# A decoder layer on one core: gates and rotary key as high and low columns of one weight unit, constant rows by SyncE, half of the rope tables in the second block

## The chip, the core and the metric

The kernel runs on one core of a Trainium2 chip. The core has a matrix engine (TensorE, PE in the rows, with its weight loads PEld), a vector engine (VectorE, DVE), an activation engine (ScalarE, ACT), a general engine (GpSimd, POOL) and SyncE (SP), which here only issues DMAs. Each engine works off its own instructions in order. The metric is the device time of one execution in microseconds (us): the median of three runs of the kernel before is 2408.57 us (2407.36 to 2414.97).

## The reference, cut to what matters

One layer on 2048 tokens of width 1024, all in float32. Only the token mixer's first part is touched by the change:

```
a    = rmsnorm(x, g)
proj = a @ w_in          # columns: qk 512, v 512, o 512, gates 8, c_q 256, c_kv 128, k_r 32
gates = proj[gates] + b_gates                     # input and forget gates of 4 mLSTM heads
h_ml  = mlstm(silu(conv(qk)), v, gates) ...       # recurrent over chunks
k_rope = rope(k_r, cos, sin)                      # one rotary key, shared by 8 heads
q, k  = [nope | rope] per head from c_q, c_kv     # then causal attention, 8 heads
out   = x + norm(mix @ w_out) ...  then the MLP
```

rope(x1, x2) is (x1 cos - x2 sin, x1 sin + x2 cos) on the two 16-wide halves of the 32 values.

## The kernel before, in words

**Float32 in three products.** TensorE multiplies in the type fp32r. A float32 factor is split into a high part (its value rounded to fp32r, by an ACT copy) and a low part (what is left, by a subtraction). A product of two such factors is three matmuls into one PSUM bank: high by high, high by low, low by high (`mm3`, lines 252 to 255, which is why nearly all matmuls have the lines L253, L254, L255).

**The projection** runs in four blocks of 512 tokens. A block goes through units of 128 columns of w_in: 13 to 15 are the latents, 0 is a mixed unit, 1 to 4 the conv inputs, 5 to 8 the values, 9 to 12 the output gates, 16 to 18 the second projections of the latents (k, v, q and rotary q). Unit 0 holds 8 gate columns, 56 zero columns, 32 columns of the rotary key, and the same 32 with their halves exchanged. Eight steps k of mm3 (24 matmuls) fill its PSUM bank; `stabiliser` (line 960 on) takes it out as the tile G (128 x 512), transposes the 8 gate rows with four small matmuls (`gp`, L976) and starts the mLSTM's gate arithmetic. `rotate` (lines 921 to 959) multiplies the rotary key rows with the rope tables: a load of the table tile tg, three DVE operations (POOL in block 0), an ACT rounding, one more subtraction, two stores to krd in DRAM.

**Weights.** In block 0 a unit's raw columns are loaded (tile wr), split into wh and wl, and wl is stored to DRAM (wparts). In later blocks most units load wr and wl, and only wh is computed again, by ACT (`wload`).

**Rope tables** are computed on DVE and ACT in two halves (`rope_tables`, L1361 to L1392): half 0 serves blocks 0 and 2, half 1 blocks 1 and 3. `RB`, `RK` name the operation after which a half's positions are loaded; before, both start behind the last x tile of block 0.

**Towards attention.** The last block's four mLSTM chunks (num, hn, ht) run while the first attention work starts: score maxima m of head 0 need the tiles QK (row parts loaded from DRAM: qkd, qrd, krd), then the scores S with one more row, number 96, that is constant (one for K, zero for the low parts). These rows are loaded by DMAs that POOL issues (L1496, L1498) from the input `edge`, once for each of two QK tiles. POOL also fills the ones column of V (L1487, L1492) and a 65-column matrix onecol (L1493, L1494), and computes the pow of the mLSTM's norm (sm, L1289), the weighted q (qs, L1235) and some low parts of the probabilities (pl, L1668).

**Order.** A planner (`Plan.run`) simulates all operations with estimated costs, keys and buffer rings, and emits them in its order; on PE, ACT, DVE and POOL that order is pinned. On SP it is the order of issue. So an edit of one operation's cost or place moves many rows near it.

Of the kernel before, what the change touches and what calls it, by code (L numbers as in the profile page):

```python
# [54 lines left out]
OB = 1  # L55
QLO = 0
# [35 lines left out]
RB = (0, 0)  # L92
RK = (7, 7)
# [151 lines left out]
def trunk(ctx: ExitStack, tc: tile.TileContext, x, xT, pos, wu, wout, wup, wdn, cols, rows, consts, edge, out, dbg=None):  # L245
# [39 lines left out]
    identr = top.tile([P, P], F32R, tag="identr", name="identr")  # L285

# [4 lines left out]
    qrd = dram.tile([2, P, 2, SEQ], F32, tag="qrd", name="qrd")  # L291
    krd = dram.tile([32, 2, SEQ], F32, tag="krd", name="krd")
# [24 lines left out]
    for name, bufs in (  # L317
        ("awr", WR), ("wh", 5), ("wl", 5), ("mma", 1), ("mmb", 1), ("pst", 1), ("chh", 1), ("sg", SG), ("cbc", 1), ("G", GB_), ("raw", 2), ("cy", 2), ("cth", 2),
        ("rsbc", 2), ("tg", 1), ("R", 1), ("aS", 2), ("E", 2), ("iwbc", 1), ("qs", 1), ("num", 1), ("kv", 1), ("kw", 1), ("hn", HN),
        *((f"x{x}{k}", 2 if k < XDB else 1) for k in range(KD) for x in "hl"),  # L320
    ):
        pl.ring(name, bufs)
# [23 lines left out]
    mrow = b1.tile([1, 20], F32, tag="mrow", name="mrow")  # L346
    cst8 = [b1.tile([P, 129], F32, tag=f"C{p}", name=f"C{p}") for p in range(2)]
# [39 lines left out]
    o_rest = pl.op("SP", 1000, load_rest, [o_fill], key=kA(0, 16), kb=70)  # L387

    def fills2():
        for p in range(2):  # L390
            pool.memset(cst8[p], 0.0)
        pool.memset(vext[:, :, :, 128:129], 1.0)

# [3 lines left out]
    o_fill2 = pl.op("Pool", 900, fills2, key=kA(0, -40))  # L397
    pl.op("Activation", 600, masks, [o_rest], key=kA(1, 0))
# [46 lines left out]
    def wload(b, u):  # L445
# [10 lines left out]
        def place_l():  # L456
            t["l"] = wp.tile([P, 1024], F32R, tag="wl", name=f"wl{b}_{u}", bufs=5)
# [14 lines left out]
        o_turn[:] = [gl]  # L472
# [4 lines left out]

    def wsplit(b, u):
        if b > STB[u]:
# [16 lines left out]
        def lo(s):  # L496
            if s.start == 0:
                t["l"] = wp.tile([P, 1024], F32R, tag="wl", name=f"wl{b}_{u}", bufs=5)
# [38 lines left out]
    def unit(b, u):  # L537
# [5 lines left out]
        def mm(k):  # L543
            if k == 0:
                t["p"] = psm.tile([P, TB], F32, tag=t["at"], name=f"mm{b}_{u}")
            s = slice(k * P, (k + 1) * P)
            mm3(t["p"], w["h"][:, s], w["l"][:, s], *tiles[b, k], k == 0, k == KD - 1)

        last = None
        for k in range(KD):  # L550
            last = pl.op(
                "PE", PIN, lambda k=k: mm(k), [w["op"][k], *o_x[b, k]] + ([last] if k else behind), kA(b, TIME[b][u] + (FILL if k and fill else 0.0)),
# [371 lines left out]
    def rotate(b, t, G):  # L924
# [4 lines left out]
        def load():  # L929
            t["tgr"] = e2.tile([P, TB], F32R, tag="cth", name=f"tg{b}")  # L930
            t["tg"] = f32(t["tgr"])
            dma(t["tg"][64:128], trigd[:, b * TB : (b + 1) * TB])
# [18 lines left out]
        g = pl.op("SP", 500, load, [o_rope[b % 2], G], key, take=("cth",), kb=128)  # L951
        o = pl.op(*cost, d1, [g, G], key)
# [9 lines left out]
    def stabiliser(b):  # L962
# [10 lines left out]
        def gates():  # L973
            t["p"] = pst.tile([P, 512], F32, tag="tr", name=f"gp{b}")
            for c in range(4):
                pe.transpose(t["p"][:, c * 8 : c * 8 + 8], t["G"][0:8, c * P : (c + 1) * P], ident[0:8, 0:8])  # L976
# [104 lines left out]
        h = pl.op("PE", 330, gates, [G, o_cst], key, take=("pst",), free=[("G", G)])  # L1081
# [352 lines left out]
    a2 = av = ar2 = pq = pS = po = onecol = maskneg = None  # L1434
# [25 lines left out]
    def switch3():  # L1460

        nonlocal av, ar2, pS, po, onecol
# [8 lines left out]
        onecol = av.tile([P, P], F32R, tag="onecol", name="onecol")[:, 0:65]  # L1471
# [16 lines left out]
    for s in (0, "v", 1):  # L1488

        def fill(s=s):  # L1490
            if s == "v":
                pool.memset(f32(V[1][:, :, :, 128:129]), 1.0)  # L1492
                pool.memset(f32(onecol[:, 0:64]), 0.0)  # L1493
                pool.memset(f32(onecol[:, 64:65]), 1.0)  # L1494
            else:
                pool.dma_start(Kh[s][96:97, :], edge[0:1])  # L1496
                for z in (Kl, Ql):
                    pool.dma_start(z[s][96:97, :], edge[1:2])  # L1498

        o_const[s] = pl.op("Pool" if s == "v" else "SP", 490 if s == "v" else 1500, fill, [o_s3 if s else o_s1], key=EKEY - 30 if s == 0 else -50, kb=0 if s == "v" else 24)  # L1500
# [1186 lines left out]
def prepare(inputs):  # L2687
# [8 lines left out]
    z = np.zeros((DM, 56), np.float32)  # L2696
    misc = np.concatenate([w[:, 1536:1544], z, kr, kr[:, 16:], kr[:, :16]], axis=1)
# [68 lines left out]
```

## Time and profile before

| | us |
|---|---|
| median of 3 runs | 2408.57 (2407.36 to 2414.97) |
| the profiled execution's own time | 2408.7 |
| its span, first to last instruction | 2406.9 |
| PE busy in the span | 2360.4 (98%) |
| DVE, ACT, POOL busy | 1732.2, 1361.8, 815.3 |
| mean granted TensorE clock | 0.995 of full speed |
| mean DMA rate | 187 GB/s |

The projection takes about the first 480 us of the span, the change over to attention the next 60, attention, output projection and MLP the rest. A matmul's row gives the time from its start to a modelled end; matmuls overlap, so the distance from one start to the next is shorter than the duration in the row. A row of a timeline has the start, the duration (with "x8" that of eight merged instructions), engine, line, operation, output and inputs, and in brackets the idle time of the engine before it and what ended that. A row of the windows view has a stretch, its length, each engine's busy time in it, the granted clock, the DMA share and GB/s.

### The profile page before, as it was taken

The page shows a single profiled execution, that of the slowest core. Times are in us where ns is not written, and L with a number is a line of the kernel's source. Part 1 is how long each engine was busy: PE and PEld are TensorE (multiplying, and loading weights), DVE is VectorE, ACT ScalarE, POOL GpSimd, SP SyncE. Part 2 cuts the span into 40 slices and gives each one's busy share as a digit, 9 for nine tenths or more (in the row PEclk, how much of TensorE's full clock was granted, in tenths as well). Part 3 has the DMA queues.
Part 4 walks back from the last instruction along what each step waited for, and adds up shares of the span by engine and source line. Part 5 has one row for each costly group of instructions (what it writes and reads, how often), then busy time and mean ns, then how long its engine had stood idle before and what let it go on. Part 6 is the DMA issues. An engine that isn't in the chain of part 4 may idle for free. (4 is left out here: it accounts for less than half of the span.)

```text
span 2406.9 us, 34273 instructions
## 1 busy us (share of the span) xinstructions
PE 2360.4 (98%) x11141; PEld 1904.2 (79%) x11141; DVE 1732.2 (72%) x3105; ACT 1361.8 (57%) x2644; POOL 815.3 (34%) x698
## 2 busy tenths in 40 slices
PE   9999999989999999999999999999999999999997
PEld 7777878767777777788788888888888888888885
DVE  6867665658888888647767677766675677776777
ACT  5646454437778877444666556655564344433454
POOL 2725242538788888422000000000000223222346
PEclk9999999999999999999999999999999999999998
DMA  8697979886222321567777797665674445445358
GB/s 288 217 336 248 351 249 335 267 197 152 54 56 54 81 57 32 160 225 249 243 214 221 226 310 221 203 171 167 191 218 139 147 135 181 124 149 164 127 140 164
DMA packets 341308, 449.22 MB, mean 187 GB/s; under 512 B 34908, under 2 KB 227432, under 8 KB 341128
## 3 DMA queue, kind: packets, MB, share of 16 engines
q1 hardware_dynamic: 337192, 440.16, 58.7%
q0 software_dynamic: 3936, 6.87, 2.0%
q8 instruction: 88, 1.44, 0.3%
q14 instruction: 92, 0.75, 0.1%
HBM read 295.97 MB, written 153.05 MB: 187 GB/s over the span
## 5 line engine op out<-in xcount | busy, mean ns | idle before, releaser
L2575 POOL TENSOR_TENSOR y<-vd_0X,y 128x512 f32<-128x512 f32 x7 | 10.6, 1519 | 726.5 <-ACT vd_0X L2572 726.5
L1660 ACT ACTIVATE ph<-S 128x512 fp32r<-128x512 f32 (+1 forms) x320 | 170.3, 532 | 86.7 <-PE S L255 49.9
L1695 POOL TENSOR_TENSOR t<-t,ph 128x512 f32<-128x512 f32 (+1 forms) x192 | 212.9, 1109 | 17.3 <-ACT ph L1660 6.8
L2487 ACT CAST hh<-hr 128x512 fp32r<-128x512 f32 (+1 forms) x208 | 116.2, 567 | 157.0 <-PE d_5X L2538 15.4
L1668 DVE TENSOR_TENSOR pl<-S,ph 128x512 fp32r<-128x512 f32 (+3 forms) x271 | 156.4, 589 | 31.8 <-ACT S L1664 28.9
L253 PE MATMUL mm<-xh,wh 128*128 128x512 f32 x384 | 156.5, 408 | 4.2 <-DVE gate L1185 2.2
L2492 DVE TENSOR_TENSOR hl<-hr,hh 128x512 fp32r<-128x512 f32 (+1 forms) x208 | 133.0, 646 | 30.0 <-ACT hh L2487 23.5
L1601 DVE TENSOR_REDUCE mp<-m 128x1 f32<-128x512 f32 (+2 forms) x208 | 135.7, 666 | 25.2 <-PE m L1594 20.7
L254 PE MATMUL mm<-xl,wh 128*128 128x512 f32 x384 | 150.4, 392 | 0.8 <-DVE xl L424 0.8
L255 PE MATMUL mm<-xh,wl 128*128 128x512 f32 x384 | 150.3, 392 | 0.5 <-DVE wl L499 0.5
L1664 ACT ACTIVATE S<-S 128x512 f32<-128x512 f32 (+3 forms) x271 | 140.2, 517 | 0.4
L253 PE MATMUL S<-QK 97*128 97x512 f32 (+1 forms) x320 | 120.5, 377 | 2.1 <-DVE pl L1668 1.9
L1681 PE MATMUL o<-ph,V 128*128 128x512 f32 (+1 forms) x320 | 119.0, 378 | 1.8 <-DVE ot L1754 1.5
L1684 PE MATMUL o<-pl,V 128*65 128x512 f32 (+1 forms) x320 | 116.0, 363 | 3.4 <-POOL pl L1668 3.4
L1594 PE MATMUL m<-QK 96*128 96x512 f32 (+3 forms) x320 | 115.6, 388 | 1.8 <-DVE mp L1601 1.1
L254 PE MATMUL S<-QK 97*128 97x512 f32 (+1 forms) x320 | 116.9, 365 | 0.0
L255 PE MATMUL S<-QK 97*128 97x512 f32 (+1 forms) x320 | 116.7, 365 | 0.0
L253 PE MATMUL op<-wo,hh 128*128 128x512 f32 x256 | 100.9, 394 | 1.4 <-DVE osm L1985 1.0
L255 PE MATMUL op<-wo,hl 128*128 128x512 f32 x256 | 99.8, 390 | 0.0
L254 PE MATMUL op<-wo,hh 128*128 128x512 f32 x256 | 99.7, 389 | 0.0
L2326 ACT ACTIVATE t<-t 128x512 f32<-128x512 f32 x96 | 60.7, 632 | 65.0 <-DVE t L2321 64.6
L253 PEld LDWEIGHTS mm<-xh,wh 128*128 128x128 f32 x384 | 72.1, 188 | 22.8 <-DVE gate L1185 3.3
(6451 smaller groups left out, 7483.4 us busy)
## 6 DMA issues: line engine op xcount, KB each, us to landing
hr<-hd SPq DMA_DIRECT2D x100, 448.0 KB
wr<-in_wu_dram SPq DMA_DIRECT2D x71, 512.0 KB
hd<-t SPq DMA_DIRECT2D x128, 256.0 KB
hd<-ts SPq DMA_DIRECT2D x96, 256.0 KB
wl<-wparts SPq DMA_DIRECT2D x45, 512.0 KB
QK<-qkd SPq DMA_DIRECT2D x32, 512.0 KB
xt<-in_x_dram SPq DMA_DIRECT2D x28, 512.0 KB
xf<-xd SPq DMA_DIRECT2D x40, 256.0 KB
```

The costliest lines, as they stand in the source:

```text
L253: pe.matmul(o, ah, bh, start=start, stop=False)
L254: pe.matmul(o, ah, bl, start=False, stop=False)
L255: pe.matmul(o, al, bh, start=False, stop=stop)
L1601: vec.tensor_reduce(mp["t"][:, j, kb : kb + 1], ps[:, :n], axis=AX.X, op=ALU.max)
L1660: act.activation(t["h"][:, :w], t["S"][:, :w], AF.Exp)
L1664: act.activation(t["p"][:, :w], t["S"][:, :w], AF.Exp)
L1668: (pool if by_pool else vec).tensor_tensor(t["l"][:, :w], t["p"][:, :w], f32(t["h"][:, :w]), ALU.subtract)
L1681: pe.matmul(o0, v[:, 0:128], t["h"][:, :w], start=start, stop=stop)
L1684: pe.matmul(o1, v[:, 64:129], t["l"][:, :w], start=start, stop=stop)
L1695: pool.tensor_tensor(to, to, hv, ALU.add)
L2487: act.copy(t["h", m][:, :w], t["r", m][:, :w])
L2492: vec.tensor_tensor(t["l", m][:, :w], t["r", m][:, :w], f32(t["h", m][:, :w]), ALU.subtract)
```

## The change

Unit 0 now has the columns: gates (8), gates again (8), 48 zeros, rotary key (32), rotary key again (32). Its one weight tile carries the high part in the first copy and the low part in the second (`wboth`: columns 8 to 15 and 96 to 127 are overwritten by the remainder). Each step k is two matmuls, weight by high x and weight by low x. The rows of the two copies are then added: for the gates within the transposing matmul, whose right factor `both8` (16 x 8) is two identities one above the other; for the rotary key by an ACT copy of G[96:128] to G's partner rows and an addition. The exchange of halves is now made by two DMAs from G to G. In block 0 the combined tile is stored to wparts, later blocks load it in one piece, with no raw load and no ACT split for this unit.

The constant rows are issued by SP, from a DRAM copy `edged` of the input, ahead of the other loads of each QK tile. onecol is filled at the start, the second V's ones (`VONE`) later in the plan. Half 1 of the rope tables starts behind the first x tile of block 1.

```diff
-RB = (0, 0)
-RK = (7, 7)
+RB = (0, 1)
+RK = (7, 0)
...
+    onecol = top.tile([P, 65], F32R, tag="onecol", name="onecol")
+    edged = dram.tile([2, SEQ], F32, tag="edged", name="edged")
...
+    o_both = pl.op("DVE", 70, lambda: vec.tensor_tensor(both8, ident[0:16, 0:8], ident[0:16, 8:16], ALU.add), [o_cst], key=kA(0, 10))
...
+        pool.memset(f32(onecol[:, 0:64]), 0.0)
+        pool.memset(f32(onecol[:, 64:65]), 1.0)
...
+    o_edge = pl.op("SP", 500, lambda: dma(edged, edge), key=kA(0, 30))
...
+    def wboth(b):
...
+        def hi():
+            t["h"] = wp.tile([P, 1024], F32R, tag="wh", name=f"wh{b}_0", bufs=5)
+            act.copy(t["h"], t["r"])
+
+        def lo():
+            h, r = (x.rearrange("p (k c) -> p k c", c=P) for x in (t["h"], t["r"]))
+            for m in (slice(8, 16), slice(96, 128)):
+                vec.tensor_tensor(h[:, :, m], r[:, :, m], f32(h[:, :, m]), ALU.subtract)
...
+        if b:
+            g = pl.op("X", 0, place, o_turn, kA(b, at - LLEAD), take=("wh",))
+            d = pl.op("SP", 500, lambda: dma(f32(t["h"]), wparts[0]), [g, *o_parts[0]], kA(b, at - LLEAD), kb=512)
...
+            if u == 0:
+                for i in range(2):
+                    pe.matmul(t["p"], w["h"][:, s], tiles[b, k][i], start=k + i == 0, stop=(k, i) == (KD - 1, 1))
+                return
...
+        def move():
+            t["tgr"] = e2.tile([P, TB], F32R, tag="cth", name=f"tg{b}")
+            t["tg"] = f32(t["tgr"])
+            act.copy(t["tg"][s], t["G"][96:128])
+
+        def add():
+            eng.tensor_tensor(t["G"][s], t["G"][s], t["tg"][s], ALU.add)
+
+        def swap():
+            dma(t["G"][96:112], t["G"][80:96])
+            dma(t["G"][112:128], t["G"][64:80])
...
-        g = pl.op("SP", 500, load, [o_rope[b % 2], G], key, take=("cth",), kb=128)
-        o = pl.op(*cost, d1, [g, G], key)
+        g = pl.op("Activation", 570, move, [o_rope[b % 2], G], key, take=("cth",))
+        a = pl.op(*cost, add, [g], key)
+        w = pl.op("SP", 1000, swap, [a], key, kb=64)
+        l = pl.op("SP", 500, load, [o_rope[b % 2], a], key, kb=128)
+        o = pl.op(*cost, d1, [l, w], key)
...
-                pe.transpose(t["p"][:, c * 8 : c * 8 + 8], t["G"][0:8, c * P : (c + 1) * P], ident[0:8, 0:8])
+                pe.matmul(t["p"][:, c * 8 : c * 8 + 8], t["G"][0:16, c * P : (c + 1) * P], both8, start=True, stop=True)
...
-                pool.memset(f32(onecol[:, 0:64]), 0.0)
-                pool.memset(f32(onecol[:, 64:65]), 1.0)
             else:
-                pool.dma_start(Kh[s][96:97, :], edge[0:1])
+                dma(f32(Kh[s][96:97, :]), edged[0:1])
                 for z in (Kl, Ql):
-                    pool.dma_start(z[s][96:97, :], edge[1:2])
+                    dma(f32(z[s][96:97, :]), edged[1:2])
...
-    misc = np.concatenate([w[:, 1536:1544], z, kr, kr[:, 16:], kr[:, :16]], axis=1)
+    misc = np.concatenate([w[:, 1536:1544], w[:, 1536:1544], z, kr, kr], axis=1)
```

PE loses 32 instructions (10573 rows become 10541). Three places show how the rows move. The first is PE in unit 0 of block 0 (mm_0 is the unit's PSUM tile, xh and xl the high and low tiles of x, the first number behind them the step k). Before:

```order
L638 MATMUL rp_427<-cst,rsx_410 128x128 x4
L253 MATMUL mm_0_435<-xh_0_258,wh_0_381 128x512
L254 MATMUL mm_0_435<-xl_0_264,wh_0_381 128x512
L255 MATMUL mm_0_435<-xh_0_258,wl_0_391 128x512
L253 MATMUL mm_0_435<-xh_1_262,wh_0_381 128x512
L254 MATMUL mm_0_435<-xl_1_269,wh_0_381 128x512
L255 MATMUL mm_0_435<-xh_1_262,wl_0_391 128x512
```

and of the change:

```order
L684 MATMUL rp_434<-cst,rsx_417 128x128 x4
L591 MATMUL mm_0_442<-xh_0_263,wh_0_388 128x512
L591 MATMUL mm_0_442<-xl_0_269,wh_0_388 128x512
L591 MATMUL mm_0_442<-xh_1_267,wh_0_388 128x512
L591 MATMUL mm_0_442<-xl_1_274,wh_0_388 128x512
```

One of three matmuls is gone in each of eight steps, in each of four blocks.

The second place is POOL from the last rotary query (rs) to the first low part of the probabilities (pl). Before:

```order
L907 TENSOR_TENSOR rs_3_4735<-rt_1_4741,rs_3_4735 128x512
L1496 DMA QK_4791<-in_edge_dram 1x16x128
L1498 DMA QK_4791<-in_edge_dram 1x16x128 x2
L1235 TENSOR_TENSOR qs_1_4808<-qT_115,iwbc_1_4652 128x256
L1289 TENSOR_TENSOR sm_0_4805<-sm_0_4805,mhalf 128x4
...
L1289 TENSOR_TENSOR sm_3_5067<-sm_3_5067,mhalf 128x4
L1496 DMA QK_5188<-in_edge_dram 1x16x128
L1498 DMA QK_5188<-in_edge_dram 1x16x128 x2
L1492 MEMSET V_5186 128x64
L1493 MEMSET onecol 128x64
L1494 MEMSET onecol 128x1
L1668 TENSOR_TENSOR pl_0_0_5232<-p_0_0_5217,ph_0_0_5204 128x512
```

and of the change:

```order
L953 TENSOR_TENSOR rs_3_4714<-rt_1_4720,rs_3_4714 128x512
L1294 TENSOR_TENSOR qs_1_4784<-qT_118,iwbc_1_4619 128x256
L1348 TENSOR_TENSOR sm_0_4781<-sm_0_4781,mhalf 128x4
...
L1348 TENSOR_TENSOR sm_3_5046<-sm_3_5046,mhalf 128x4
L1550 MEMSET V_5165 128x64
L1727 TENSOR_TENSOR pl_0_0_5208<-p_0_0_5193,ph_0_0_5180 128x512
```

The DMAs and the two fills of onecol are gone from between; one fill of V stands ahead of the first pl still.

The third place is SP at the first of the two QK tiles (E and iwbc are loads for the mLSTM chunks, maskneg a constant). Before:

```order
L916 DMA qrd<-rs_3_4735 256x1x512
L1207 DMA E_2_4859<-wd_4339 128x512
L1485 DMA maskneg<-in_consts_dram 128x512
L1540 DMA QK_4791<-krd 32x2x512 x4
L1546 DMA QK_4791<-qkd 64x4x512
L1548 DMA QK_4791<-qrd 16x2x512 x2
L1215 DMA iwbc_2_4861<-wd_4339 64x2x128 x2
```

and of the change:

```order
L962 DMA qrd<-rs_3_4714 256x1x512
L1266 DMA E_2_4838<-wd_4310 128x512
L1274 DMA iwbc_2_4845<-wd_4310 64x2x128 x2
L1543 DMA maskneg<-in_consts_dram 128x512
L1552 DMA QK_4770<-edged 1x2048
L1554 DMA QK_4770<-edged 1x2048 x2
L1599 DMA QK_4770<-krd 32x2x512 x4
L1605 DMA QK_4770<-qkd 64x4x512
L1607 DMA QK_4770<-qrd 16x2x512 x2
```

Three one-row loads now stand ahead of the loads that the first score maxima need, and the chunk's iwbc moved in front of them. From the last block's rotary query products on, the order of PE is the same in both kernels, and on POOL it differs only by the rows shown.

45 lines of the change are left out of this document (33 added, 12 removed).

## The prediction

> **What bounds the kernel now.** I read the page first, then busy time by stretches of 60 us, then what PE waited for, and last the timelines around its two longest waits.
>
> ```profile
> PE 2360.4 (98%) x11141; PEld 1904.2 (79%) x11141; DVE 1732.2 (72%) x3105; ACT 1361.8 (57%) x2644; POOL 815.3 (34%) x698
> ```
>
> ```profile
> 60.00:120.00 60.00, 55.60 (x319) 43.64 (x319) 53.41 (x95) 40.72 (x93) 42.70 (x35) 1.00 0.69 216
> ...
> 180.00:240.00 60.00, 60.00 (x339) 47.84 (x337) 41.67 (x78) 37.01 (x83) 33.62 (x30) 1.00 0.74 245
> 240.00:300.00 60.00, 60.00 (x293) 48.88 (x292) 38.44 (x90) 25.44 (x43) 17.54 (x14) 1.00 0.98 355
> ...
> 480.00:540.00 60.00, 52.15 (x291) 39.37 (x290) 32.45 (x81) 21.26 (x64) 20.25 (x27) 0.91 0.83 192
> ```
>
> PE is the bound nearly everywhere (the first number behind the length). In the projection's middle it never rests, although the DMA share is 0.98, so matmuls that go there shorten the time one for one as long as loads keep up. Two stretches differ: 60 to 120, where PE rests 4.4 us beside a DVE that is busy 53 of 60, and 480 to 540, where it rests 7.9 us and its clock is not whole. What ended the rests (PE's waits up to 560 us):
>
> ```profile
> PE num L1241 <- DVE hn L1295: 3.0, 1, 3.0
> PE o L1684 <- POOL pl L1668: 3.0, 1, 3.0
> ```
>
> The two of 3 us lie in the last stretch. Cut by stretches just there:
>
> ```profile
> 481.72:484.75 3.03, 0.00 (x0) 0.00 (x0) 0.76 (x2) 0.00 (x0) 2.19 (x3) 1.00 0.59 179
> 484.75:488.82 4.07, 4.07 (x19) 3.38 (x20) 0.93 (x4) 0.48 (x3) 0.00 (x0) 0.58 0.91 231
> ...
> 521.38:524.35 2.97, 0.00 (x0) 0.00 (x0) 1.63 (x5) 0.00 (x0) 2.92 (x7) 0.75 1.02 232
> 524.35:530.09 5.74, 5.74 (x22) 4.49 (x23) 2.19 (x4) 1.17 (x2) 0.00 (x0) 0.54 1.12 201
> ```
>
> Each rest is followed by a stretch at a lower granted clock, 0.58 and 0.54, which costs 4.07 x 0.42 = 1.7 and 5.74 x 0.46 = 2.6 us more. So the first wait (A) costs 4.7 us, the second (B) 5.6 us. The shorter rests between 60 and 120 us leave the clock at 1.00. What POOL does there:
>
> ```profile
> 480.44 0.75 POOL L1496 DMA_DIRECT2D QK<-in_edge_dram  x1 [6.32 <-DMA maskneg<-in_consts_dram]
> ...
> 482.87 1.04 POOL L1289 TENSOR_TENSOR sm<-sm,mhalf 128x4 f32<-128x4 f32 x1
> ...
> 521.25 0.59 POOL L1496 DMA_DIRECT2D QK<-in_edge_dram  x1 [10.71 <-DVE mp L1601]
> ...
> 523.02 1.27 POOL L1668 TENSOR_TENSOR pl<-p,ph 128x512 fp32r<-128x512 f32 x1
> ```
>
> POOL stands at the head of its queue for the memory of a QK tile to come free, 6.3 us and 10.7 us, then issues the constant rows. Behind them stand the pow (sm), whose result DVE needs to empty num, and the low part pl. Their inputs were there long before:
>
> ```profile
> 477.39 0.16 DVE L1285 SCALAR_TENSOR_TENSOR sm<-sm 128x4 f32<-128x4 f32 x1 [0.58 <-ACT jk L1279]
> ...
> 483.94 0.76 DVE L1295 TENSOR_TENSOR hn<-num,sm 128x256 f32<-128x256 f32 x2 [3.75 <-POOL sm L1289]
> ```
>
> ```profile
> 518.03 0.59 ACT L1664 ACTIVATE p<-S 128x512 f32<-128x512 f32 x1
> ```
>
> **The change, part by part.** *Matmuls.* 4 blocks x 8 steps lose one matmul each, 32. What is one worth? Not the 392 ns of its group's row:
>
> ```profile
> L255 PE MATMUL mm<-xh,wl 128*128 128x512 f32 x384 | 150.3, 392 | 0.5 <-DVE wl L499 0.5
> ```
>
> ```profile
> 29.67 0.39 PE L255 MATMUL mm<-xh,wl 128*128 128x512 f32 x1
> ...
> 34.43 0.39 PE L255 MATMUL mm<-xh,wl 128*128 128x512 f32 x1
> ```
>
> These are the first and last of 22 matmuls in a row: 21 steps in 4.76 us, 0.227 us from start to start. 32 x 0.227 = **7.3 us less**.
>
> *Gates.* The transpose becomes a plain float32 matmul, four a block:
>
> ```profile
> 38.09 0.41 PE L976 MATMUL gp<-cst,G 8*128 8x8 f32 x4
> ```
>
> ```profile
> 34.72 1.95 PE L684 MATMUL ssp<-ones,sq 128*128 128x1 f32 x16
> ...
> 459.44 0.71 PE L1203 MATMUL S<-qT,kT 64*128 64x128 f32 x8
> ```
>
> Four transposes are four rows, 0.41 us. Eight plain float32 matmuls (ssp) are sixteen rows and 1.95 us, four of S eight rows and 0.71 us. So four plain ones cost 0.7 to 1.0 us: 0.3 to 0.6 a block, 1.2 to 2.3 in all. I take the middle, as neither row has 16 partitions: **1.7 us more**.
>
> *Wait B.* With no DMA on POOL, pl can start when p is there, 518.62, and ends at 519.9; PE wants it at 521.38. One fill of V stays ahead of pl, as the order above shows; whether it must stand for the same memory is a rival below. PE then runs on into 5.7 us of work that DVE follows easily (2.2 of 5.74 busy). I take all of it: **5.6 us less**; the lower end is 1.5, if pl starts right behind the release at 521.25 and the fill.
>
> *Wait A.* The pow can start at 477.6, hn is done by 479.5, num runs at 481.7. But what is late next? PE comes 4.7 us sooner to the first maxima, which did not wait before. They need QK:
>
> ```profile
> 490.21 0.22 PE L1594 MATMUL m<-QK 96*128 96x128 f32 x1
> ```
>
> ```profile
> 479.84 2.57 SPq L1540 DMA_DIRECT2D QK<-krd  x4
> 482.45 0.60 SPq L1546 DMA_DIRECT2D QK<-qkd  x1
> 483.09 1.24 SPq L1548 DMA_DIRECT2D QK<-qrd  x2
> 484.44 1.27 SPq L1215 DMA_DIRECT2D iwbc<-wd  x2
> ...
> 540.48 0.26 SPq L1765 DMA_DIRECT2D sumd<-ou  x1
> ```
>
> ```profile
> 488.97 0.73 POOL L1235 TENSOR_TENSOR qs<-qT,iwbc 128x256 f32<-128x256 f32 x1 [5.06 <-DMA iwbc<-wd]
> ```
>
> The iwbc issued right behind landed 3.3 us after its issue ended (485.71 to 488.97), so the last part of QK landed at about 487.6. SP now issues three constant rows first, at 0.26 us (the one-row sumd) to 0.6 us (the others) each: 0.8 to 1.8 us later, 488.4 to 489.4. PE comes at 485.5, so it stands again, for 2.9 to 3.9 us, and the maxima start 0.8 to 1.8 us sooner than before. A rest of that length has cost 1.7 us of clock each time here. Net: between 1.8 gained and 0.9 lost; and 4.7 gained if QK lands in time after all. I take **0**, since the iwbc row is the nearest there is.
>
> The Trainium skill, TensorE: Matmul & The Clock Gate, in Part 1 on the HAM clock gate, says the clock halves after an idle window of about 3.4 us that runs free of the kernel. The trace halved it after rests of 3.03 and 2.97, which agrees if the modelled ends of matmuls shorten the rests by some tenths. By that rule a new rest of 2.9 may fall short of a window; wait A would then bring up to 1.8 us instead of 0, and the time would be 2394.7.
>
> *Block 0.* Half 1 of the rope tables leaves a stretch in which DVE is the busiest engine; POOL gets one addition.
>
> ```profile
> L1378 DVE SCALAR_TENSOR_TENSOR ang<-kk,ang 128x512 f32<-128x512 f32 x6 | 8.3, 1384 | 0.1
> ...
> L1387 ACT ACT_TABLE_LOAD x2 | 2.6, 1283 | 0.0
> ...
> L937 POOL TENSOR_TENSOR G<-G,tg 32x512 f32<-32x512 f32 x1 | 1.3, 1288 | 0.2 <-DMA tg<-trigd 0.2
> ```
>
> The three costliest operations of one half are 4.2 us of DVE, and one half has a table load of 1.3 us on each side of its sine. PE's 4.4 us of rest can shrink at most to 0, and can grow by POOL's 1.3 us. I take 1.5 less. In block 1 the same work lies beside DVE at 42 of 60 and a PE that never rests: I take 0.5 more, at worst 2. Together **1 us less**.
>
> *Hidden.* The rotary chain grows by an ACT copy, a DVE addition and two DMAs on SP:
>
> ```profile
> L946 ACT CAST tg<-G x4: 616/616/618, 108.3 to 436.5; 32x512 fp32r<-32x512 f32 x4
> L959 SPq DMA_DIRECT2D krd<-G x4: 313/318/1077, 110.3 to 443.2; - x4
> L937 DVE TENSOR_TENSOR G<-G,tg x3: 683/683/683, 176.4 to 419.0; 32x512 f32<-32x512 f32 x3
> ```
>
> With 3.3 us for the DMAs to land, that is 0.6 + 0.7 + 1.2 + 3.3, some 6 us. The last krd store is at 443.2 and the load of krd at 479.84: 36 us of cover. The three later blocks lose a load of 512 KB and an ACT split each, which only eases SP and ACT.
>
> Sum: -7.3 + 1.7 - 5.6 + 0 - 1.0 = -12.2. The profiled execution took 2408.7 us (span 2406.9), 0.1 from the median of 2408.57. Forecast: **2396.5 us**.
>
> **Rivals.** (1) *QK is in time*: SP's short loads cost next to nothing and the earlier iwbc makes room; wait A goes whole, 4.7 more: 2391.8. For it: PE did not wait at 490.21, so the true landing is unknown. Against it: the iwbc row. (2) *Wait B stays*, so the change does not do what it says: the fill of V waits for the same release (521.25), pl with its 1.27 us ends at 522.7 at the earliest and B brings 1.5 of 5.6: 2400.6; with nothing from block 0 either, 2401.6. For it: V and QK of that stage are opened together. Against: V's ones are a small part, and the DMA waited for all of QK's ground. (3) *Slower: SP stands.* The swap DMAs wait at the head of SP's queue for the addition, and behind them stand the next block's weights and x. In block 0 the addition is POOL's, whose rotary operations lay 10 us apart:
>
> ```profile
> 93.96 1.29 POOL L937 TENSOR_TENSOR G<-G,tg 32x512 f32<-32x512 f32 x1 [0.21 <-DMA tg<-trigd]
> ...
> 103.95 2.14 POOL L940 TENSOR_TENSOR tg<-G,tg 32x512 f32<-32x512 f32 x1
> 104.80 1.04 SPq L416 DMA_DIRECT2D xr<-in_xT_dram  x1
> ```
>
> If SP stands 10 us in block 0 and 5 in each later one, where DMA is near full, and nothing covers it, 25 us come on top: 2421. It decides from 12.2 + 7.2 = 19 us on. Against: PE never rests between 180 and 300 us although SP has such waits today, and the loads that go give SP slack.
>
> **How the numbers follow.** Forecast 0.52, QK in time 0.20, wait B stays 0.20, SP stands 0.06, 0.02 for others. What a measurement of this kernel can tell from no change is about 0.3%, 7.2 us: faster means under 2401.3. The forecast's case is all but 0.04 under it, rival 1 wholly, rival 2 half: faster 0.78, same 0.16, slower 0.06. The forecast's own range, from the bounds of its terms (gates 0.6 each way, A from 1.8 gained to 0.9 lost, blocks 0 and 1 from 4 gained to 3 lost), is 2392 to 2401; to 2390.5 it takes in rival 1, to 2403.5 rival 2.
>
> **What would show it.** Right: unit 0 with 16 matmuls at 0.227 us; no POOL wait of 6 and 10 us; pl ended before PE wants it, with no rest of PE there and a whole clock behind it; a rest of about 3 us at the first maxima on a DMA; eight gp rows of 0.7 to 1.0 us. Wrong: pl still behind a release, new rests of PE on weights in blocks 1 to 3, or rests in block 0 on POOL.

## The result and the profile after

The changed kernel is **slower**: 2427.64 us (median of six runs, 2424.27 to 2432.23) against 2410.09 us of the kernel before (six runs), a ratio of 1.0071 with a 95% interval of 1.0056 to 1.0086. The forecast was 2396.5 us with a range of 2390.5 to 2403.5; it missed by 31 us and on the wrong side. The profiled execution took 2432.2 us (span 2430.2).

The page's first part, then PE's waits up to 600 us (lines of unchanged code stand 2 to 59 further down than before: L253 became L255, L1594 became L1653):

```profile
PE 2383.0 (98%) x11125; PEld 1903.0 (78%) x11125; DVE 1731.8 (71%) x3110; ACT 1358.5 (56%) x2645; POOL 810.5 (33%) x693
```

```profile
PE mm L255 <- DVE gate L1244: 4.4, 2, 3.6
PE m L1653 <- DMA iwbc<-wd: 3.2, 1, 3.2
PE kt L1311 <- DVE C L1327: 2.8, 1, 2.8
...
PE S L255 <- DVE pl L1727: 1.1, 1, 1.1
```

PE issued fewer matmuls and was busy 22.6 us *longer* (2360.4 before); the time it stood still is the same, 47 us. The two waits of 3 us at num and o are gone, and three others of about that size have come. But where is a busy PE slower? Stretches of 60 us, after (the same ones as shown of before):

```profile
60.00:120.00 60.00, 57.75 (x328) 45.25 (x328) 48.75 (x88) 39.93 (x93) 43.23 (x36) 1.00 0.72 240
...
180.00:240.00 60.00, 56.81 (x318) 44.10 (x316) 45.39 (x81) 35.84 (x81) 32.55 (x29) 0.97 0.72 241
240.00:300.00 60.00, 59.47 (x285) 47.95 (x283) 37.69 (x89) 25.50 (x43) 16.48 (x14) 1.00 0.95 342
...
480.00:540.00 60.00, 54.92 (x317) 41.78 (x316) 34.73 (x87) 23.74 (x67) 18.23 (x20) 0.97 0.79 191
```

These account for little: at 564 us, in the first steps of the attention, the changed kernel is 1.3 us behind. It still is at 995 us. Three stages that the diff doesn't touch follow, and it falls behind steadily. Starts of the same matmuls in the two traces (the 97th of 768 of the output projection, which begins at 952.29 between the last attention steps; the first of the second unit of up; the first of down):

```
                     before     after    difference
output projection    995.02    996.33      +1.30
MLP up              1171.37   1174.57      +3.20
MLP down            1771.58   1781.06      +9.48
end                 2406.85   2430.24     +23.39
```

PE's busy time, matmuls, clock, DMA share and GB/s in 100 us of the MLP down stage, before and then after:

```profile
2000.00:2100.00 100.00, 99.95 (x441) 1.00 0.51 159
```

```profile
2000.00:2100.00 100.00, 100.00 (x432) 1.00 0.49 156
```

PE never rests, the clock is whole in both, the DMA moves nearly the same, and each matmul takes 0.2315 instead of 0.227 us from start to start. The same instructions in the same order have become 2% slower. So there are two questions: what slows the later stages by 22 us, and why the projection is 1.3 us behind instead of 12 us ahead.

### The profile page after: what moved, and what is told of

It reads as the page before. It is cut to its first block, busy times and chain, and to the rows that moved or that the text cites. A ratio compares the mean times of both kernels' runs of the same rounds, so it can differ in the third digit from the quotient of the medians.

```text
span 2430.2 us, 34234 instructions
## 1 busy us (share of the span) xinstructions
PE 2383.0 (98%) x11125; PEld 1903.0 (78%) x11125; DVE 1731.8 (71%) x3110; ACT 1358.5 (56%) x2645; POOL 810.5 (33%) x693
## 4 chain that ended last, share of the span: by engine, by line
PE 55%; DVE 1%; DMA 0%; issue 0%; ACT 0%; POOL 0%; DVEq 0%; SPq 0%; POOLq 0%; ACTq 0%
PE op L255 1%; PE op L257 1%; PE op L256 1%; PE d_2X L2596 1%; PE d_4X L2596 1%; PE d_1X L2596 1%; PE d_3X L2596 1%; PE d_1X L2598 1%; PE d_4X L2598 1%; PE d_2X L2598 1%; PE d_3X L2598 1%; PE d_3X L2597 1%; PE d_4X L2597 1%; PE d_2X L2597 1%; PE d_1X L2597 1%; PE d_5X L2596 1%
## 5 line engine op out<-in xcount | busy, mean ns | idle before, releaser
L255 PE MATMUL mm<-xh,wh 128*128 128x512 f32 x352 | 144.1, 409 | 6.8 <-DVE gate L1244 4.4
L256 PE MATMUL mm<-xl,wh 128*128 128x512 f32 x352 | 138.7, 394 | 0.8 <-DVE xl L433 0.8
L257 PE MATMUL mm<-xh,wl 128*128 128x512 f32 x352 | 138.4, 393 | 0.5 <-DVE wl L541 0.5
L255 PE MATMUL S<-QK 97*128 97x512 f32 (+1 forms) x320 | 120.3, 376 | 3.2 <-DVE pl L1727 3.0
L1653 PE MATMUL m<-QK 96*128 96x512 f32 (+3 forms) x320 | 115.7, 388 | 5.0 <-DMA iwbc<-wd 3.2
L255 PE MATMUL op<-wo,hh 128*128 128x512 f32 x256 | 101.9, 398 | 1.2 <-DVE x L2055 0.8
L255 PEld LDWEIGHTS mm<-xh,wh 128*128 128x128 f32 x352 | 66.4, 189 | 24.2 <-DVE gate L1244 5.2
```

What stands on the lines that cost most here:

```text
L255: pe.matmul(o, ah, bh, start=start, stop=False)
L256: pe.matmul(o, ah, bl, start=False, stop=False)
L257: pe.matmul(o, al, bh, start=False, stop=stop)
```

## Experiments on the later stages: where the tiles lie

The one thing that the change alters for these stages is the place of their tiles. `onecol`, 65 columns, moved from a pool that is opened late into the pool `top`, under everything on the left side of the memory. `top` grew from 1792 to 2080 bytes a partition, and every left tile behind it moved by 288 bytes; tiles on the right side stayed. From the compiled program's addresses I took, for each matmul of 512 columns, where its moving and its stationary operand start within 256 bytes, and from the trace of the changed kernel the mean time to the next start:

```
stage    moving, stationary (mod 256)    steps   mean ns to next start
op       128, 160                          369   233.3
op       160, 160                          364   227.8
up       128, 128                         1611   227.6
up       128, 160                          753   233.1
up       160, 128                          186   233.3
up       160, 160                           97   228.2
down     160, 128                         1529   232.5
down     128, 128                         1142   231.5
before, all three: 128, 128               6048   226.8 to 227.3
```

Where the two start at the same place the step is 227 to 228 ns, else 233. In down the equal pairs are slow too: most of them stand in runs of three between unequal ones, and equal pairs in runs of three take 231.7 ns in up as in down, those in runs of more than 15 in up 227.4. (The units of the projection, mm, have equal places in both kernels and keep their step, 228.8 and 229.0 ns.) My first theory was that a shift by 32 within 64 bytes costs; the rival, that the matmuls are slow for another reason.

**e1**, the changed kernel with 32 bytes more in `top`; **e2**, the kernel before with 32 unused bytes there; **e3**, the same at both ends:

```diff
e1:
-    onecol = top.tile([P, 65], F32R, tag="onecol", name="onecol")
+    onecol = top.tile([P, 80], F32R, tag="onecol", name="onecol")[:, 0:65]
e2:
     identr = top.tile([P, P], F32R, tag="identr", name="identr")
+    top.tile([P, 8], F32, tag="pad", name="pad")
e3: e2 and, behind the pool top,
+    ctx.enter_context(tc.tile_pool(name="rpad", bufs=1, side="right")).tile([P, 8], F32, tag="rpad", name="rpad")
```

> The changed kernel with one line altered: the tile onecol is 80 columns wide of which 65 are used, so that it takes 320 bytes of each partition instead of 288 and every tile placed behind it starts at a multiple of 64 bytes from the tiles of the other side of the memory again, as before the change. Theory A (the shift by 32 bytes slows the matmuls of the output projection and the MLP): the pitch of the down matmuls falls from 232 back to 227 ns, and the 22 us that the changed kernel lost between 995 us and its end come back: 2403 to 2409 us, at 0.997 to 1.000 of the kernel before, since the two stood only 1.3 us apart at the start of the output projection. Theory B (the matmuls run slower for another reason: clock, memory traffic, the chip's state, other instructions around them): 2424 to 2432 us as the changed kernel, pitch 231 to 233 ns.

> The kernel before with one line added: an unused tile of 32 bytes per partition in the pool top, which shifts the tiles behind it by 32 bytes and changes no instruction. Theory A: slower by 20 to 23 us, 2428 to 2434 us (ratio 1.008 to 1.010), the loss in the output projection (about 1 us), up (6 us) and down (14 us), the projection and the attention as before. Theory B: no change, 2407 to 2415 us (ratio 0.998 to 1.002).

> The kernel before with 32 unused bytes per partition at both ends of the memory, so that the tiles of both sides move by 32 bytes and both operands of every matmul of the output projection and the MLP start at 32 over a multiple of 64. Theory A1 (what costs is that the two operands of a matmul start at different places within 64 bytes): no loss, 2407 to 2415 us. Theory A2 (what costs is any start off a multiple of 64): a loss at least that of the run with one side shifted, 2430 to 2440 us. Theory B: no change.

e2, no instruction changed and 32 bytes that nobody uses: 2431.38 us, **1.0093** (1.0080 to 1.0105). That is more than the whole loss of the changed kernel (17.6 us). The 100 us of its down stage:

```profile
2000.00:2100.00 100.00, 100.00 (x432) 1.00 0.50 155
```

But e1 is as slow (2429.65 us, 1.0087, 1.0072 to 1.0102), and so is e3 (2429.15 us, 1.0078, 1.0064 to 1.0092), so the theory in its first form fell. In e1 the left side has moved by 320 bytes, 64 over a multiple of 256; in e3, since right tiles grow downwards, the two sides moved apart by 64. Their unequal pairs in op and up take 233.2 to 233.4 ns (moving 128 and stationary 192, 96 and 160; 230.6 where it is the other way round). So 64 bytes apart costs as 32 does, and the period is longer.

**e5**, the changed kernel with `top` at 2048 bytes; **e6**, **e18**, the kernel before with 128 and 256 unused bytes on the left; **e7**, with 32 on the left and 224 on the right:

```diff
e5:
-    mhalf = top.tile([P, 16], F32, tag="mhalf", name="mhalf")[:, 0:8]
+    ones_half = top.tile([P, 80], F32R, tag="onecol", name="onecol")
+    onecol, mhalf = ones_half[:, 0:65], f32(ones_half)[:, 72:80]
     identr = top.tile([P, P], F32R, tag="identr", name="identr")
-    onecol = top.tile([P, 65], F32R, tag="onecol", name="onecol")
e6, e18: e2's line with [P, 32], with [P, 64]
e7: e3's lines with [P, 8] on the left, [P, 56] on the right
```

> The changed kernel with onecol and mhalf in one tile of 320 bytes, so that the pool top is 2048 bytes, 256 more than the 1792 before (instead of 288 or 320 more); no instruction changes. Theory A (a matmul is slower where its moving and its stationary operand start at different places within 128 bytes, which is what separates 227 from 233 ns in the traces of e1 to e3): all pairs of the output projection, up and down are equal again within 256 bytes, the pitch there is 227 ns, and 20 to 22 us come back: 2405 to 2411 us. Theory A3 (any move of the left side against the right costs): 2425 to 2433 us. Theory B (not the place, but the instructions of the changed kernel): excluded by e2 already.

> The kernel before with 128 unused bytes in top; each pair of operands of the output projection, up and down then differs by 128 within 256 bytes for the part of the matmuls whose two operands lie on different sides (about half of the output projection and of up, nearly all of down), and by nothing within 128. Theory A with a period of 128 bytes: no loss, 2407 to 2415 us. Theory A with a period of 256: a loss as in e2, 2427 to 2433 us.

> The kernel before with 32 unused bytes on the left side and 224 on the right, whose tiles grow downwards: every operand of the output projection and the MLP starts at 32 over a multiple of 128, and the two of a matmul at the same place within 256. Theory A1 (only the difference between the two operands counts): no loss, 2407 to 2415 us. Theory A2 (the start of each operand off a multiple of 64 or 128 counts): a loss of 20 us or more, 2427 to 2440 us.

> The kernel before with 256 unused bytes in top: the control to e2 (32 bytes) and e6 (128 bytes). Theory A with a period of 256 bytes: no loss, 2407 to 2413 us, the ratio's interval holds 1. If any move of the left side costs: 2427 to 2433 us.

The same 100 us of the down stage in e6, then in e7, in e18 and in e5:

```profile
2000.00:2100.00 100.00, 100.00 (x432) 1.00 0.49 154
```

```profile
2000.00:2100.00 100.00, 99.95 (x441) 1.00 0.51 160
```

```profile
2000.00:2100.00 100.00, 99.95 (x441) 1.00 0.50 156
```

```profile
2000.00:2100.00 100.00, 99.95 (x442) 1.00 0.49 156
```

```
run      left   right   down: moving, stationary mod 256   median us   ratio (95%)
e2        +32     0     160,128 and 128,128                  2431.38   1.0093 (1.0080-1.0105)
e3        +32   -32     160, 96 and  96, 96                  2429.15   1.0078 (1.0064-1.0092)
e6       +128     0       0,128 and 128,128                  2428.41   1.0076 (1.0061-1.0090)
e7        +32  -224     160,160                              2409.99   1.0002 (0.9993-1.0011)
e18      +256     0     128,128                              2410.00   0.9995 (0.9986-1.0004)
```

e7 excludes that each operand's own place counts, as far as one place can: all start at 160 instead of 128, and nothing is lost. e6 excludes a period of 128; e5 and e18 show that 256 costs nothing. **What counts is the difference of the two starts modulo 256 bytes**; 32, 64 and 128 cost alike, 192 and 224 too (the pairs the other way round in e1 to e3); other differences were not measured. e5 is the changed kernel without this effect: 2407.97 us, 0.9991 (0.9982 to 0.9999), some 20 us below e1 and the changed kernel. Its gain over the kernel before is 1.5 us, not 12.

## Experiments on the projection: why 1.5 us and not 12

In the table, e5 against the kernel before, from the starts of the same matmuls in the two traces, beside the forecast's terms (the gates' 1.7 us spread over the four blocks). Traces of kernels with the same instructions differed by up to 4 us at 995 us (changed kernel and e1), so a stretch's single figure is rough; the two profiled executions are 0.6 us apart, the medians -1.5.

```
stretch                                      forecast    e5
up to the unit in block 0                        0      +0.7
the unit, four times                            -7.3    -7.8
rest of block 0                                 -1.1    -0.6
rest of block 1                                 +0.9    +4.4
rest of block 2                                 +0.4    +1.4
block 3 to the o that waits for pl (A and B)    -5.2    +0.5
behind it, to the first steps of attention       0      +0.9
to the end                                       0      +1.2
```

**Block 1.** VectorE in the changed kernel:

```profile
197.24 0.68 DVE L981 TENSOR_TENSOR G<-G,tg 32x512 f32<-32x512 f32 x1
...
202.87 2.74 DVE L993 TENSOR_TENSOR G<-G,tg 32x512 f32<-32x512 f32 x1 [1.91 <-DMA tg<-trigd]
...
207.78 0.60 DVE L1327 SCALAR_TENSOR_TENSOR C<-C,sp,kv 128x129 f32<-128x129 f32 x2
```

The rotary key's first product waits at the head of VectorE's queue for the table that is loaded behind the addition; the rest of the chain follows, and then the update of the memory's C, for which PE stands. What the rest costs, in stretches (PE's busy time first, the clock third from the end):

```profile
205.70:208.52 2.82, 0.01 (x1) 0.03 (x1) 2.72 (x7) 0.98 (x3) 0.50 (x1) 1.00 0.62 238
208.52:211.37 2.85, 2.85 (x8) 1.81 (x9) 2.05 (x7) 2.75 (x11) 0.53 (x1) 0.56 0.46 79
437.93:441.51 3.58, 0.01 (x2) 0.00 (x1) 2.87 (x4) 1.71 (x4) 2.26 (x3) 0.93 0.74 214
441.51:444.23 2.72, 2.72 (x6) 2.15 (x7) 2.18 (x3) 0.60 (x1) 2.10 (x2) 0.50 0.43 132
488.35:491.58 3.23, 0.00 (x1) 0.03 (x1) 0.00 (x0) 1.27 (x6) 0.00 (x0) 1.00 1.04 229
491.58:495.73 4.15, 4.15 (x13) 3.18 (x14) 1.12 (x5) 1.28 (x4) 1.26 (x2) 0.59 1.03 213
```

**Block 3** is the second pair, and VectorE has the same chain ahead of the gate's evacuation there:

```profile
434.04 1.68 DVE L993 TENSOR_TENSOR G<-G,tg 32x512 f32<-32x512 f32 x1
435.75 1.67 DVE L996 TENSOR_TENSOR tg<-G,tg 32x512 f32<-32x512 f32 x1
437.45 1.65 DVE L999 TENSOR_TENSOR G<-G,tg 32x512 f32<-32x512 f32 x1
439.78 0.95 DVE L1005 TENSOR_TENSOR G<-G,tg 32x512 fp32r<-32x512 f32 x1 [0.68 <-ACT tg L1002]
440.76 0.69 DVE L1244 TENSOR_TENSOR gate<-mm,rsbc 128x512 f32<-128x512 f32 x1
```

PE had finished that unit at 437.9 and stands until 441.5. **e4** and **e8** put the chain's steps on GpSimd in all blocks, on e1 and on e5:

```diff
-KPOOL = (0,)
+KPOOL = (0, 1, 2, 3)
```

> The changed kernel with onecol padded as in e1, and the rotary key's element-wise steps of blocks 1 to 3 on GpSimd instead of VectorE (KPOOL = (0, 1, 2, 3); the four changed steps and the last subtraction). If the longer rotary chain, standing on VectorE ahead of the memory's C (block 1) and of the gate's evacuation (block 3), is what makes TensorE stand 2.81 and 3.58 us there, both stands go, and with them about 1.3 us each of matmuls at half clock: 5 to 9 us below e1, 2395 to 2403 us. Rival: GpSimd, at about 1.35 us a step, becomes the late one (kw, E and the chunk's squares wait for it): between 2 us below and 5 us above e1.

> e5 with the rotary key's element-wise steps of blocks 1 to 3 on GpSimd. In e4 against e1 this took away TensorE's stands behind VectorE (2.81 and 3.58 us) and brought 4 us at the start of the output projection, though the stand at the first maxima grew from 2.81 to 6.42 us. Expected: 2 to 5 us below e5, 2401 to 2408 us, that is 0.997 to 0.999 of the kernel before. Rival: the 4 us lie within what two profiles of one kernel differ by, and the time is that of e5.

Both stands are gone. At the unit 11 of block 3, e8 is 5.0 us ahead of the kernel before, where e5 is 4.0 behind. But the time is not better: e8 2409.81 us (0.9995, 0.9987 to 1.0004), e4 2431.77 (1.0089, 1.0076 to 1.0102); both times lie where the rivals had them. The planner's order has changed with the move, and a lead at one unit is not a lead in all the work: num of the chunk ahead of the maxima starts at 475.9 us in e8 and at 475.1 in e5. At the first maxima PE then waits for their QK loads, 6.31 us in e8 and 6.42 in e4. SyncE now has one chunk's E more ahead of these loads and stands 4.5 us for it in e8 (until PE's num), so that the krd loads are issued at 486.23, in e5 at 480.60. So the gain was lost again, in part ahead of the maxima and in part at them.

**e9** and **e10** are the two parts alone: the unit in two products with its rotary chain and gates, and the constant rows with `onecol` (in e5's tile) and the rope tables.

```diff
e9: the changed kernel, with
-RB = (0, 1)
-RK = (7, 0)
+RB = (0, 0)
+RK = (7, 7)
    and edged, o_edge, fill and onecol as before
e10: the kernel before, with edged, o_edge, fill and the onecol of e5, and
-RB = (0, 0)
-RK = (7, 7)
+RB = (0, 1)
+RK = (7, 0)
```

> The kernel before with one part of the change: the unit with gates and rotary key in two products, its weights, the gates by fp32 matmul and the longer rotary chain; constant rows, rope tables and onecol as before (so no tile of the later stages moves). As the prediction priced this part: 7.3 us of matmuls less and 1.7 us of gates more, 2403 to 2405 us. Theory V (the longer rotary chain stands on VectorE ahead of the C update in block 1 and of the gate's evacuation in block 3, where the aligned change shows TensorE idle for 1.23 to 2.81 and 3.56 us and then some matmuls at half clock): most of the 7 us is given back, 2406 to 2411 us.

> The kernel before with the other part: constant rows by SyncE, onecol filled at the start (in the 320-byte tile with mhalf, so that the left side moves by 256), the rope table's half in block 1; the unit in three products as before. As the prediction priced it: 5.6 us of the wait at o, 1.5 us in block 0, 0.5 us more in block 1, nothing from the wait at num because the QK loads are late next: 2402 to 2404 us. Rival: the wait at o moves on too (the aligned change stands 1.86 us for pl at S right behind), 2404 to 2408 us.

Both are slower than the kernel before, by 0.1 to 0.2%: e9 2413.22 us, 1.0011 (1.0002 to 1.0020); e10 2414.68 us, 1.0018 (1.0009 to 1.0027). That is against every expectation (theory V of e9 had the loss in other places, below), and the two don't add up to e5, which is faster than either. VectorE of e10 in block 1, with the old, shorter rotary chain, and PE's longest wait up to 600 us:

```profile
211.26 0.68 DVE L943 TENSOR_TENSOR G<-G,tg 32x512 f32<-32x512 f32 x1 [5.38 <-DMA tg<-trigd]
...
214.06 0.60 DVE L1274 SCALAR_TENSOR_TENSOR C<-C,sp,kv 128x129 f32<-128x129 f32 x2
```

```profile
PE kt L1258 <- DVE C L1274: 4.2, 1, 4.2
```

So block 1's stand needs no new rotary step: the rotary key of block 1 uses the very half of the tables that the change makes in block 1. **e13** puts that half back into block 0, on e5:

```diff
-RB = (0, 1)
-RK = (7, 0)
+RB = (0, 0)
+RK = (7, 7)
```

> e5 (the change with its tiles at multiples of 256) with the second half of the rope tables made in block 0 as before (RB = (0, 0), RK = (7, 7)). In e10, the rows and tables alone, VectorE stands 5.38 us in block 1 at the rotary key's first step for the table's load (G L943 behind tg from trigd), the memory's C update queues behind it, and TensorE stands 4.18 us for that C. If it is the table's new place that costs this: the stand of 1.23 to 2.81 us at kt in block 1 goes with the half-clock matmuls behind it, block 1 gains 4 to 5 us, block 0 loses its 1.5 us again: 2 to 4 us below e5, 2404 to 2406 us. Rival: the longer rotary chain does it, and e5's time stays (2406 to 2410 us).

The stand at kt goes, but the time grows, against both expectations: 2412.71 us, 1.0011 (1.0003 to 1.0020). PE of e13 in block 0:

```profile
57.60 0.35 PE L1132 MATMUL tp<-cst,R 16*128 16x16 f32 x3
61.30 0.79 PE L255 MATMUL kp<-ch,wh 128*128 128x512 f32 x1 [3.35 <-ACT ch L783]
64.57 0.79 PE L256 MATMUL kp<-cl,wh 128*128 128x512 f32 x1 [2.47 <-POOL cl L786]
```

With the cheaper unit and the tables in block 0, the planner orders the first key products ahead of the v products, before their input is there; in e5 v products stand at this place. The same stands are in e9. In the runs with these parts, what block 1 adds behind its unit, and block 0 behind its own, against the kernel before:

```
                                       rest of block 0                     rest of block 1
tables in block 1, chain on VectorE    e5 -0.6, e12 -0.3, e15 0.0,         e5 4.4, e12 5.9, e15 4.7,
                                       e17 -0.5                            e17 4.5
  the same, with the old unit          e10 -0.4                            e10 7.9
tables in block 1, chain on GpSimd     e4 -0.4, e8 -0.3, e11 0.1           e4 2.5, e8 2.5, e11 1.8
tables in block 0                      e9 9.1, e13 7.7, e14 8.9, e16 8.9   e9 2.3, e13 2.4, e14 2.4, e16 2.4
```

With the new unit and the chain on VectorE, making the tables late costs 2 to 4 us in block 1 (7.9 with the old unit); with the tables in block 0, the new unit costs 8 to 9 us there, by the planner's order.

**The first maxima.** e11 and e12 leave the QK loads where they were and put the maxima 8 us (on e8) and 4 us (on e5) later in PE's order:

```diff
e12 (e11 and e17: -152.0 and 8.0):
-EKEY = -160.0
+EKEY = -156.0
-            load_qk(h, qb, keys[h, qb, "m"][0] - LDK)
+            load_qk(h, qb, keys[h, qb, "m"][0] - LDK - (0 if h or qb else 4.0))
```

The keys EKEY - 30 of the mask, the constant rows and the rotary keys became EKEY - 34 (EKEY - 38).

> e8 (aligned, rotary steps on GpSimd) with the four first row maxima 8 us later in TensorE's order, behind the products of the last v unit, and their QK loads where they were on SyncE (EKEY = -152, the loads' keys lowered by 8). If in e8 the whole gain of the projection went into the stand of 6.31 us at the first maxima, and the products that now come ahead of them fill it: 4 to 7 us below e8, 2402 to 2406 us. Rival: the maxima are then late for the first attention steps, and the stand moves there: 2407 to 2413 us.

> e5 (aligned, rotary steps on VectorE) with the first maxima 4 us later in TensorE's order, their loads where they were. If its stand of 2.92 us there is filled by the products behind: 2 to 4 us below e5, 2403 to 2406 us. Rival: the time is set by the maxima's chain, not by TensorE's order: as e5, 2406 to 2410 us.

e12: **2401.88 us, 0.9967** (0.9958 to 0.9976), 6 us below e5 and a little below what was expected; e11: 2403.25 us, 0.9970 (0.9958 to 0.9981). The stand at the first maxima is gone from both, so it was lost time. **e14** to **e17** combine: e14 is e12 with the tables in block 0, e15 is e12 with block 3's chain on GpSimd (`KPOOL = (0, 3)`), e16 has both, e17 is e15 with the maxima 8 us later.

> e12 (first maxima 4 us later) with the second half of the rope tables in block 0 as before. If the two are independent: 2 to 4 us below e12, 2398 to 2400 us. Rival: an earlier TensorE in block 1 meets the next wait (QK loads or block 3's gate), and e12's time stays, 2400 to 2403 us.

> e12 with the rotary steps of block 3 on GpSimd (KPOOL = (0, 3)), so that VectorE's four steps and the subtraction no longer stand ahead of the gate's evacuation, for which TensorE waits 3.56 us in e12 at 441 us. If that stand and its half-clock matmuls are lost time: 3 to 5 us below e12, 2397 to 2399 us. Rival: the QK loads or the r products of block 3 (stand 2.48 us at q in e11, 2.14 at r in e8) take it: within 2 us of e12.

> Both: e12 with the rope tables' second half in block 0 and block 3's rotary steps on GpSimd. Added up from the two expectations: 2394 to 2398 us. Rival: the projection is then bound by the chain from the last key products to the QK loads, and the time is that of the better of e14 and e15.

> e15 (block 3's rotary steps on GpSimd) with the first maxima 8 instead of 4 us later. In e15 TensorE no longer stands at the gate (444 us) but 2.41 us at the first maxima for the QK loads, and the two times are the same. If the QK loads are what takes the gate's gain, more products ahead of the maxima fill that stand: 2 to 3 us below e15, 2401 to 2403 us. Rival: the stands behind it (1.02 us at m for mp, 2.36 at o for ot in e15) grow by as much, and e15's time stays, 2403 to 2406 us.

e14 (2409.88 us, 1.0002, 0.9993 to 1.0010) and e16 (2409.79 us, 1.0004, 0.9995 to 1.0013) lose in block 0 as e13 does; against the expectation. e15 (2404.12 us, 0.9976, 0.9968 to 0.9985) takes the gate's stand away and gets nothing for it: PE comes early to the maxima again (PE's waits from 400 us on, the second longest):

```profile
PE m L1653 <- DMA iwbc<-wd: 2.4, 1, 2.4
```

e17 puts more products ahead of them, and the gate's time is saved too: **2399.16 us, 0.9958** (0.9943 to 0.9974), the fastest, 11.9 us below the kernel before. That lies inside the forecast's range, but e17 has three edits that the forecast kernel had not (the padding, block 3's chain on GpSimd, the later maxima), so it does not bear the sum out. Its page and its longest waits up to 600 us:

```profile
PE 2355.8 (98%) x11125; PEld 1898.8 (79%) x11125; DVE 1724.2 (72%) x3105; ACT 1362.0 (57%) x2645; POOL 820.8 (34%) x698
```

```profile
PE m L1653 <- DVE mp L1660: 3.7, 4, 2.2
PE kt L1311 <- DVE C L1327: 1.5, 1, 1.5
```

## Why the prediction was wrong, step by step

*The sum as a whole* failed first: it took every stage behind 530 us at its time of before. The diff's line that moves `onecol` into `top` got no term, as a tile without cost, and it costs 20 to 22 us of the 31 (e2 alone, e5 in reverse). Nothing in the profile of before shows this; its operands all start alike. The other 9 to 11 us are in the terms below.

*Matmuls, -7.3:* right. Sixteen in a row in block 0, whose first and last start 3.52 us apart, 0.235 us each (PE's timeline after); the four units together took 7.8 us less in e5's trace than before.

```profile
27.30 0.48 PE L591 MATMUL mm<-xh,wh 128*128 128x512 f32 x1
...
30.82 0.39 PE L591 MATMUL mm<-xl,wh 128*128 128x512 f32 x1
```

*Gates, +1.7 (1.2 to 2.3):* a little above its range, 2.6. They are eight rows, and the next matmul starts 0.98 to 0.99 us behind the first, against 0.34 for the transposes (38.09 to 38.43 before), 0.64 more in each block. The same timeline:

```profile
38.39 1.05 PE L1035 MATMUL gp<-both,G 16*128 16x8 f32 x8
39.38 0.50 PE L255 MATMUL mm<-xh,wh 128*128 128x512 f32 x1
```

*Wait A, 0:* the place and the length of the new wait came as forecast, the zero not. num no longer waits, and PE stands 3.23 us at the first maxima (2.9 to 3.9 were forecast) with the clock at 0.59 behind it, in the third pair of stretches above. Rival 1 (QK in time) did not come. But the length is partly luck: PE came at 488.35 instead of 485.5, held up by block 3's gate, and the maxima started at 491.58, not at 488.4 to 489.4, so they were 1.4 us later than before instead of 0.8 to 1.8 sooner. The last QK issue ended at 487.19, and the maxima started 4.4 us behind it, where the prediction had 3.3. The Trainium skill, TensorE: Matmul & The Clock Gate, Part 1, has an idle window of about 3.4 us that runs free of the kernel, and the prediction allowed that a rest of 2.9 might fall short of it. Here the rest of 2.82 us in block 1 too was followed by 0.56. Over the runs the length alone does not decide: 2.67 us at num in e6 was followed by 0.50, 3.13 us at the first maxima in e13 left the clock at 1.00.

*Wait B, -5.6:* mis-sized, its net is about 2 us. The wait itself is gone (pl ends at 522.99, and PE takes it at 524.22 without standing), and rival 2 did not come. By the starts of the same matmuls, the changed kernel makes up 3.1 us at this o, and 2.4 more in the whole clock behind it. But what is late next was not asked here: S then stands 1.1 us for pl and o 1.0 for ot, at 547 to 549 us, and the clock is at 0.74 to 0.77 until 556; in e5 S stands 1.86 us for pl. So 3.8 of the 5.5 us are given back, 3.3 in e5. POOL's and PE's timelines after:

```profile
521.71 1.28 POOL L1727 TENSOR_TENSOR pl<-p,ph 128x512 fp32r<-128x512 f32 x1 [8.01 <-ACT p L1723]
```

```profile
547.32 0.50 PE L255 MATMUL S<-QK 97*128 97x512 f32 x1 [1.10 <-DVE pl L1727]
...
549.29 0.47 PE L1740 MATMUL o<-ph,V 128*128 128x512 f32 x1 [1.02 <-DVE ot L1813]
```

*Block 0 -1.5, block 1 +0.5:* mis-sized, in e5 -0.6 and, with the gates and the rotary chain, +4.4. The prediction priced the tables' operations by DVE's free time in block 1 and didn't ask who reads the tables: block 1's own rotary key does, and it stands at the head of VectorE's queue until they are loaded.

*Hidden, the rotary chain:* the step that failed next to it. The 36 us of cover are those of the krd store ahead of its load; they are there. What was not named is what stands *behind* the chain's steps on their engine, now that they run later: C in block 1 (for the late table, as e10 and e13 show) and the gate's evacuation in block 3, each followed by some 3 us of PE at half clock. In block 3 the chain's first product starts at 434.04, where it started at 419.0 before; e9, with the tables of before, has this stand too (3.59 us), e10, with the old chain, has not. Of the prediction's signs of being wrong this was none.

*Rival 3, SP stands:* did not come; no wait of PE behind 16 us is for weights, and the loss that decided was elsewhere.

*The range:* the bounds of its terms add up to 2391 to 2402 us, not 2392 to 2401; nothing rests on this.

## What to carry to other kernels

A tile added to a pool is a change to every tile behind it: before pricing an edit, compare the places of both operands of the costly matmuls, modulo 256 bytes, and pad the pool to keep them. Cover is counted per queue, not per result: for each step that is added or made late, name what is issued behind it on that engine and who waits for that. And a wait taken away is worth its length only if the next input of the same engine is there, so the work behind it may have to be ordered anew (e5 to e12 to e17).

## What the runs showed of the hardware that was not expected

A stream of 512-column matmuls at whole clock runs at 227 ns a step when the moving and the stationary operand start at the same place modulo 256 bytes, and at 230 to 233 ns when they start 32, 64 or 128 apart; over the output projection and the MLP here that is 18 to 22 us. The Trainium skill, SBUF — State Buffer, under Who interferes with whom, gives TensorE two independent read ports, one for the moving operand and one for the weights, by which the one's place should not matter to the other; no run here can look into the ports, and the measured times decide: it matters. Equal pairs right behind unequal ones are slow too: 231.7 ns in runs of three, in up and in down, 227.4 in runs of more than 15 in up. So down's equal pairs, most of them in runs of three, are slow on the whole (231.5) and up's are not (227.6). Why the places matter, and which of two neighbouring matmuls' loads meet, stays open.
